# The last products of a hybrid encoder step: another order, the last tiles one by one, and their rows added by VectorE

## The chip, the core and the metric

The kernel runs on one core of one Trainium2 chip. The metric is the device time of one execution in microseconds (us); before the change the median of three runs is 2330.51 us (2329.35 to 2331.84). Five engines work side by side and meet through semaphores: PE (TensorE, matmuls, with its weight loads PEld), DVE (VectorE), ACT (ScalarE), POOL (GpSimd) and SP (SyncE, which here only issues DMAs). Sixteen DMA engines move data; SP, ACT and GpSimd issue to them through queues of their own.

## The reference

One layer of a streaming encoder. The rows are 1024 prompt frames and 8 x 16 sample frames, 1152 rows of 2048 numbers.

```python
h = rms_norm(x, norm_pre)
q_sb, k_sb, v_sb, gate_sb, q_r, k_r, v_r, gate_r = split(h @ w_in)      # 2048 x 8192
o_sb = stick_breaking(q_sb, k_sb, v_sb)       # 8 heads, strictly causal; sample frames also see 1024 cached ones
o_r, state = retention(rope(q_r), rope(k_r), v_r, state)                # 8 heads, chunks of 64
y = concat(head_rms_norm(o_sb) * silu(gate_sb), head_rms_norm(o_r) * silu(gate_r))   # rows x 2048
out = y @ w_out                                                          # 2048 x 2048
x = x + rms_norm(out, norm_post)
```

All inputs and outputs are float32. The change lies in the last two lines: the output projection and the normalised sum.

## The kernel before

**Precision.** Every large matmul is done on float32 pairs: `split` (lines 165 to 169) copies a block into a rounded "high" half on ACT and subtracts it on DVE for the "low" half. `times` (line 1162) then adds high x high, high x low and low x high into one accumulator: three matmuls per block, 128 x 128 against 128 x 512.

**Rows.** Group 0 (G0) holds row tiles 0 to 3 and the sample tile, group 1 (G1) row tiles 4 to 7. Of each group, two tiles of 128 rows are the "upper" half and two the "lower" half.

**The output projection** (from line 1153 on) multiplies 2 x 2 blocks by the seven-product form of Strassen and Winograd. `LEFT` and `RIGHT` (lines 66, 67) say which block, or which precomputed sum of blocks, each product 1 to 7 takes; the sums of weights lie in `s_b`, those of rows in `s_s`, all in HBM. `GOES` (line 69) says for each group and product what is done with its result: a triple of destination block, source block (None: plain copy on ACT), sign or third block (then two blocks are added), and 1 where the destination has its final value. C11 and C12 are the two column halves of the upper rows, C21 and C22 those of the lower rows. Each product comes in two halves, nh 0 and 1, of 512 columns. One pass has up to five accumulators: two tiles of G0, one sample tile (products 1, 2, 3 and 5 alone), two tiles of G1. For each of eight blocks `load_split` (line 1177) loads 256 KB of weights through SP into a ring of five raw buffers (`wr`) and splits them into a ring of four (`wh`, `wl`); then every accumulator takes its three matmuls.

Product 5 of G0 with the sample tile is done earlier, under the last attention heads. Then the loop at line 1335 runs products 1, 2, 6, 7, 5 (G1 alone), 3, and after it product 4. `both` and `left` (lines 1310, 295) load and split a product's left operand one or two half products ahead; `then` (line 1325) says when. G0 alternates between two kept places (`kept`, `at`), G1 between two buffers. In the first half of product 1, G1 runs two blocks behind G0 (`LAG`), since its operand is just being loaded.

**Background jobs.** Work beside the matmuls is written as generators. `tick` (line 222) advances the program's own clock by one and issues one step of one job that is due; a step ends by saying in how many ticks it wants to go on. `product` calls `tick` a given number of times after each accumulator's three matmuls: two in product 1, one later on. `drain` and `all_of` tick until a job is done. `pin` (line 185) keeps an instruction behind the last matmul issued so far (`anchor`) in the order that the scheduler makes; what is not pinned, such as `load_split`, may go ahead as far as its buffers allow. Each engine and each queue then works in its order. The jobs of this stretch are: `sums` with `sum_rows` (the row sums of G1: eight items of two loads, four subtractions on DVE and one store through ACT), `left` and `left_sample`, `load_gpost`, and `collect` (line 1209), which takes an accumulator out of PSUM by `GOES`.

**Finishing rows.** Where `GOES` marks a block as final, `complete` squares it on ACT into a column of the row's sum and multiplies it by the gain on DVE. When all four 512-column parts of a row tile are complete, `finish` (line 1298) makes the inverse root (`scale`, `inv_rms`: small steps on DVE and one root on ACT), scales each part on ACT and has `add_out` store it with an adding DMA from GpSimd: the output rows already hold x, copied there by `residuals` long before. Each part is 256 KB.

**The end.** The second half of product 4 runs three blocks for all four accumulators from the ring. The other five blocks (`KEPT`) are loaded and split into a place of their own (`kh`, `kl`), and each tile in turn takes its last five blocks from there, so that the tiles end one after the other. Each tile's last part is then subtracted, squared and scaled; parts listed in `BY_DVE` are multiplied and added to x on DVE (line 1381), with x loaded in 512-column pieces (`xr`), and stored plainly through SP (`store`, line 1283); the others are scaled on ACT and go through `add_out`.

Of the kernel before, what the change touches and what calls it, by code (L numbers as in the profile page):

```python
# [9 lines left out]
F32 = mybir.dt.float32  # L10
# [52 lines left out]
HT = KT // 2  # L63
HALF = D // 2
KEPT = 5
LEFT = {1: ("y", 0, 0), 2: ("y", 1, 0), 3: ("s", 2), 4: ("y", 1, 1), 5: ("s", 3), 6: ("s", 0), 7: ("s", 1)}
RIGHT = {1: (0, 0), 2: (1, 0), 3: (1, 1), 4: 2, 5: 0, 6: 3, 7: 1}
C11, C12, C21, C22 = (0, 0), (0, 1), (1, 0), (1, 1)
GOES = {
    0: {  # L70
        5: ((C22, None, "+", 0), (C12, None, "+", 0)), 3: ((C12, C12, "+", 1),),
        1: ((C21, None, "+", 0),), 2: ((C11, C21, "+", 1),),
        6: ((C21, C21, "+", 0), (C12, C12, C21, 0)), 7: ((C21, C21, "+", 0), (C22, C22, C21, 1)),
        4: ((C21, C21, "-", 1),),
    },
    1: {
        1: ((C21, None, "+", 0),), 2: ((C11, C21, "+", 1),), 6: ((C12, C21, "+", 0),),
        7: ((C22, C12, "+", 0), (C21, C12, "+", 0)), 4: ((C21, C21, "-", 1),), 5: ((C22, C22, "+", 1), (C12, C12, "+", 0)), 3: ((C12, C12, "+", 1),),
    },
}  # L80
CS1, CS2 = (2, 0), (2, 1)
SAMPLE_LEFT = {5: 0, 3: 1, 1: 0, 2: 1}
# [10 lines left out]
def tile_hybrid_step(  # L93
# [40 lines left out]
    def x_rows(t):  # L134
        return x_prompt[0, t * P : (t + 1) * P, :] if t < PT else xs_flat
# [29 lines left out]
    def split(hi, lo, src):  # L165
        return (
            nc.scalar.activation(hi, src, AF.Copy),  # L167
            nc.vector.tensor_tensor(lo, src, hi.bitcast(F32), ALU.subtract),  # L168
        )
# [271 lines left out]
    with ExitStack() as s1:  # L441
# [713 lines left out]
        def weights_of(n, nh, k):  # L1155
            kind = RIGHT[n]
            if isinstance(kind, int):
                return s_b[nh][k][:, kind, :]
            rows = slice((kind[0] * HT + k) * P, (kind[0] * HT + k + 1) * P)
            return w_out[0, rows, kind[1] * HALF + nh * 512 : kind[1] * HALF + (nh + 1) * 512]  # L1160

        def times(a, x, k, ts, wh, wl, first, last):
            hi, lo = x
            nc.tensor.matmul(a, hi[k][:, ts], wh, start=first, stop=False)  # L1164
            nc.tensor.matmul(a, hi[k][:, ts], wl, start=False, stop=False)  # L1165
            anchor[0] = nc.tensor.matmul(a, lo[k][:, ts], wh, start=False, stop=last)  # L1166

# [41 lines left out]
        def collect(n, nh, accs):  # L1209
            for key, a in accs:  # L1210
                g, p = (0, 0) if key == "s" else key

                def at(block):
                    return (g, 2 * block[0] + p), 2 * block[1] + nh

                for dst, src, how, last in SAMPLE_GOES[n] if key == "s" else GOES[g][n]:
                    o = area(*at(dst))
                    if src is None:
                        nc.scalar.activation(o, a, AF.Copy)
                    elif isinstance(how, str):  # L1220
                        nc.vector.tensor_tensor(o, area(*at(src)), a, ALU.add if how == "+" else ALU.subtract)
                    else:
                        nc.vector.tensor_tensor(o, area(*at(src)), area(*at(how)), ALU.add)
                    if last:
                        Job(complete(*at(dst)), D_FIN)
                    yield 1
# [14 lines left out]
    with ExitStack() as s3:  # L1241
# [18 lines left out]
        def tile_of(key):  # L1260
            return SAMPLE if key[1] == 4 else GROUPS[key[0]]["tiles"][key[1]]
# [43 lines left out]
                yield 1  # L1305
                add_out(key, c)

        at = {2: 0, 6: 1, 7: 0, 3: 1, 4: 0}

        def both(n, groups):  # L1310
            made = []
# [8 lines left out]
        def all_of(made):  # L1320
# [2 lines left out]

        G0, G1, BOTH = (0,), (1,), (0, 1)
        then = {
            (1, 1): ((2, BOTH),), (2, 1): ((6, BOTH),), (6, 0): ((7, BOTH),), (7, 0): ((5, G1), (3, G0)),
            (5, 0): ((3, G1),), (3, 0): ((4, BOTH),),
        }
        (first,) = both(1, G1)
        more = Job(sums(fp, [sum_rows(1, h) for h in range(H)], D_SUM3), 16)  # L1330
# [1 line left out]
        ready = [Job(left_sample(1, *mine["s", 1], fp, "ys", 4), 24)]  # L1332
        for p in range(4):
            outs[1, p] = rp.tile([P, D], F32, name=f"out{p}", tag=f"out{p}")
        for n, groups in ((1, BOTH), (2, BOTH), (6, BOTH), (7, BOTH), (5, G1), (3, BOTH)):
            for nh in range(2):
                if n > 1 and nh == 0:
                    all_of(ready)
                    ready = []
                if (n, nh) == (2, 1):  # L1340
                    drain(more)
                for what in then.get((n, nh), ()):
                    ready += jobs_of(both(*what))
                start = dict(feed=first, lag=LAG) if (n, nh) == (1, 0) else {}
                accs = product(n, nh, groups, n < 4, 2 if n < 2 else 1, **start)
                if (n, nh) == (2, 1):
                    phases.close()
                    xp.append(s3.enter_context(tc.tile_pool(name="xp", bufs=1)))
                Job(collect(n, nh, accs), 1)
        all_of(ready)  # L1350
        Job(collect(4, 0, product(4, 0, BOTH, False, 1)), 1)
        accs = product(4, 1, BOTH, False, 1, HT - KEPT)
        kh, kl = (half[1].rearrange("p a n -> p (a n)").rearrange("p (k n) -> p k n", k=KEPT) for half in mov)
        for k in range(KEPT):
            wr = wp.tile([P, 512], F32, name="wr3", tag="wr", bufs=5)
            nc.sync.dma_start(wr, weights_of(4, 1, HT - KEPT + k))
            split(kh[:, k], kl[:, k], wr)
        while jobs:
            tick()
        scaled = [c3.tile([P, 2, 512], F32, name=f"og{t}", tag=t) for t in ("sh", "sl")]  # L1360
        rows = {}
        BY_DVE = {(0, 0): (1,), (0, 1): (1,), (1, 0): (1, 3), (1, 1): (0, 2, 3, 1)}
        for (g, p), _ in accs:
            for c in BY_DVE[g, p]:
                x = rows[g, p, c] = xp[0].tile([P, 512], F32, name="xr", tag="xr", bufs=8)
                nc.sync.dma_start(x, x_rows(tile_of((g, 2 + p)))[:, c * 512 : (c + 1) * 512])
        for (g, p), a in accs:
            key = g, 2 + p
            for k in range(KEPT):
                k1 = HT - KEPT + k  # L1370
                times(a, mine[g, 4], k1, TS[p], kh[:, k], kl[:, k], False, k1 == HT - 1)
            o = area(key, 1)
            nc.vector.tensor_tensor(o, o, a, ALU.subtract)
            square(key, 1, o)
            t = scaled[g][:, p, :]
            nc.vector.tensor_tensor(t, o, gpost[:, 512:1024], ALU.mult)
            rs = scale(key)
            for c in (0, 2, 3, 1):
                part = t if c == 1 else area(key, c)
                if (g, p, c) in rows:  # L1380
                    nc.vector.scalar_tensor_tensor(part, part, rs, rows[g, p, c], ALU.mult, ALU.add)
                    store(key, c, nc.sync, part)
                else:
                    nc.scalar.activation(part, part, AF.Copy, scale=rs)
                    add_out(key, c)
# [104 lines left out]
```

## Time and profile before

| | |
|---|---|
| median of three runs | 2330.51 us |
| profiled execution | 2331.03 us, of which the span of instructions is 2329.3 us |
| mean granted TensorE clock | 0.992 |
| PE busy | 2264.7 us (97%), 14496 matmuls |
| DVE busy | 1231.3 us (53%) |
| ACT busy | 920.4 us (40%) |
| POOL busy | 362.7 us (16%) |
| DMA | 460.51 MB, mean 198 GB/s |

The page gives busy time by engine, then the span in 40 slices of 58 us, one digit each for tenths of busy time, then the DMA queues (q0 is GpSimd's, q1 SP's, q10 ACT's), the chain of work that ended last, and the costliest groups of instructions. Times in other views are us from the start of the span. A releaser in square brackets names what ended an engine's idle time before an instruction.

### The profile page before, as it was taken

The page shows a single profiled execution, that of the slowest core. Times are in us where ns is not written, and L with a number is a line of the kernel's source. Part 1 is how long each engine was busy: PE and PEld are TensorE (multiplying, and loading weights), DVE is VectorE, ACT ScalarE, POOL GpSimd, SP SyncE. Part 2 cuts the span into 40 slices and gives each one's busy share as a digit, 9 for nine tenths or more (in the row PEclk, how much of TensorE's full clock was granted, in tenths as well). Part 3 has the DMA queues.
Part 4 walks back from the last instruction along what each step waited for, and adds up shares of the span by engine and source line. Part 5 has one row for each costly group of instructions (what it writes and reads, how often), then busy time and mean ns, then how long its engine had stood idle before and what let it go on. Part 6 is the DMA issues. An engine that isn't in the chain of part 4 may idle for free.

```text
span 2329.3 us, 39299 instructions
## 1 busy us (share of the span) xinstructions
PE 2264.7 (97%) x14496; PEld 2045.5 (88%) x14496; DVE 1231.3 (53%) x2540; ACT 920.4 (40%) x1948; POOL 362.7 (16%) x606
## 2 busy tenths in 40 slices
PE   7999999999999999999999999999999999999995
PEld 7999999999999999998888989888888887788884
DVE  7235444353435444355556565655665666555754
ACT  6323333333333333334343334333334445334435
POOL 3002020111202020111102112020211211000004
PEclk9999999999999999999999999999999999999998
DMA  7546657575557647567677787878886767864539
GB/s 256 184 146 193 193 157 213 179 213 167 169 175 209 195 148 221 175 199 255 166 234 205 228 231 225 227 212 226 231 234 199 209 175 187 265 196 157 171 103 181
DMA packets 447073, 460.51 MB, mean 198 GB/s; under 512 B 182048, under 2 KB 310048, under 8 KB 445728
## 3 DMA queue, kind: packets, MB, share of 16 engines
q1 hardware_dynamic: 315808, 292.28, 43.3%
q0 software_dynamic: 29440, 79.72, 12.4%
q10 hardware_dynamic: 101632, 86.00, 11.8%
q8 instruction: 113, 1.85, 0.3%
q14 instruction: 80, 0.66, 0.1%
HBM read 353.02 MB, written 114.29 MB: 201 GB/s over the span
## 4 chain that ended last, share of the span: by engine, by line
PE 83%; DMA 7%; DVE 5%; ACT 3%; issue 2%; SPq 0%; POOL 0%; DVEq 0%; ACTq 0%; POOLq 0%
PE acc L371 45%; PE accn L427 17%; PE a L1165 4%; PE a L1164 4%; PE a L1166 4%; PE pa L752 2%; PE z L722 2%; PE zc L791 1%; PE pd L855 1%; DMA mr<-s_h 1%; DMA yr<-s_y 1%; DMA ro<-s_rk 1%; PE pa L900 1%; DMA s_rk<-rk 1%; DVE kp L651 1%
## 5 line engine op out<-in xcount | busy, mean ns | idle before, releaser
L371 PE MATMUL acc<-mh,wh 128*128 128x256 f32 (+2 forms) x2304 | 662.5, 340 | 0.0
L371 PE MATMUL acc<-ml,wh 128*128 128x256 f32 (+2 forms) x2304 | 658.9, 339 | 0.0
L371 PE MATMUL acc<-mh,wl 128*128 128x256 f32 (+2 forms) x2304 | 656.5, 338 | 0.0
L168 DVE TENSOR_TENSOR wl<-wr,wh 128x512 fp32r<-128x512 f32 x507 | 348.0, 690 | 487.4 <-ACT wh L167 464.8
L167 ACT ACTIVATE wh<-wr 128x512 fp32r<-128x512 f32 x507 | 319.0, 631 | 653.2 <-PE acc L371 347.3
L371 PEld LDWEIGHTS acc<-ml,wh 128*128 128x128 f32 x2304 | 421.7, 188 | 31.2 <-issue 3.3
L371 PEld LDWEIGHTS acc<-mh,wl 128*128 128x128 f32 x2304 | 424.2, 188 | 27.8
L371 PEld LDWEIGHTS acc<-mh,wh 128*128 128x128 f32 x2304 | 420.1, 188 | 31.9 <-issue 3.3
L427 PE MATMUL accn<-whn,mh 128*128 128x256 f32 x1152 | 330.5, 287 | 0.0
L427 PE MATMUL accn<-wln,mh 128*128 128x256 f32 x1152 | 326.5, 283 | 0.0
L427 PE MATMUL accn<-whn,ml 128*128 128x256 f32 x1152 | 326.0, 283 | 0.0
L427 PEld LDWEIGHTS accn<-whn,mh 128*128 128x128 f32 x1152 | 221.5, 192 | 3.2 <-issue 1.1
L427 PEld LDWEIGHTS accn<-wln,mh 128*128 128x128 f32 x1152 | 221.6, 192 | 0.8
L427 PEld LDWEIGHTS accn<-whn,ml 128*128 128x128 f32 x1152 | 221.3, 192 | 0.0
L168 DVE TENSOR_TENSOR wln<-wrn,whn 128x512 fp32r<-128x512 f32 x128 | 87.7, 688 | 147.2 <-ACT whn L167 146.0
L167 ACT ACTIVATE whn<-wrn 128x512 fp32r<-128x512 f32 x128 | 80.7, 633 | 188.3 <-PE accn L427 93.3
L615 POOL DMA_DIRECT2D be<-s_be x128 | 94.1, 741 | 146.6 <-DMA s_be<-be 123.0
L651 DVE TENSOR_TENSOR_SCAN kp<-kp 128x1152 f32<-128x1152 f32 (+4 forms) x40 | 82.7, 2067 | 52.3 <-POOL kp L640 35.7
L640 POOL TENSOR_SCALAR_AFFINE_SELECT kb<-kb 128x128 f32<-128x128 f32 x64 | 30.6, 485 | 458.1 <-ACT kb L634 455.8
L778 POOL DMA_DIRECT2D kcT<-cache_k x64 | 34.6, 545 | 422.4 <-PE pd L855 268.8
L1165 PE MATMUL a<-wl,mh 128*128 128x512 f32 x246 | 96.8, 394 | 2.4 <-DVE wl L168 2.4
L1164 PE MATMUL a<-wh,mh 128*128 128x512 f32 x246 | 96.5, 393 | 2.1 <-DVE rg L454 1.5
(241 smaller groups left out, 2999.9 us busy)
## 6 DMA issues: line engine op xcount, KB each, us to landing
wr<-w_cols SPq DMA_DIRECT2D x384, 256.0 KB, 4.4
wrn<-w_rows SPq DMA_DIRECT2D x128, 256.0 KB, 3.4
kcT<-cache_k POOLq DMA_DIRECT2D x64, 512.0 KB, 8.3
vc<-cache_v SPq DMA_DIRECT2D x64, 512.0 KB, 5.6
wr<-s_b SPq DMA_DIRECT2D x80, 256.0 KB, 3.2
br<-w_out SPq DMA_DIRECT2D x64, 256.0 KB, 5.2
s_b<-br ACTq DMA_DIRECT2D x32, 512.0 KB, 4.6
wr<-w_out SPq DMA_DIRECT2D x48, 256.0 KB, 4.2
```

The costliest lines, as they stand in the source:

```text
L167: nc.scalar.activation(hi, src, AF.Copy),
L168: nc.vector.tensor_tensor(lo, src, hi.bitcast(F32), ALU.subtract),
L371: last = nc.tensor.matmul(a[:, :m], lhs[:, j, :], rhs[w][:, j, o : o + m], start=(w == 0 and j == 0 and n == 0), stop=(w == KT // WQ - 1 a ...
L427: anchor[0] = nc.tensor.matmul(a, lhs[q][:, jj, ts], rhs[:, j, :], start=(w == 0 and j == 0 and n == 0 and t % 2 == 0), stop=(w == KT // 2 ...
L615: q.dma_start(raw[32 * i : 32 * i + 32, :].rearrange("p (k a) -> p k a", a=32), s[:, :, 32 * i : 32 * i + 32].rearrange("k (j b) a -> b (k ...
L651: nc.vector.tensor_tensor_scan(rev, rev, rev, 1.0, ALU.mult, ALU.bypass)
L722: nc.tensor.matmul(z[:, :c], q2[a][:, i * P : (i + 1) * P], k2[b][:, s : s + c], start=(m == 0), stop=(m == 2),)
L752: nc.tensor.matmul(po[:, :P], at[:, j, :], vn[:, j, :], start=(j == 0), stop=(j == t))
L778: ready.append((kc, nc.gpsimd.dma_start(kc, cache_k[h, m // 4, m % 4])))
L1164: nc.tensor.matmul(a, hi[k][:, ts], wh, start=first, stop=False)
L1165: nc.tensor.matmul(a, hi[k][:, ts], wl, start=False, stop=False)
L1166: anchor[0] = nc.tensor.matmul(a, lo[k][:, ts], wh, start=False, stop=last)
```

## The change

The products now run in the order 1, 2, 5 (G1 alone), 3, 6, 7, 4, with the same table `GOES` for both groups; the finality marks move accordingly, so that C12 is final with product 6. `then` and `at` follow the new order. The ticks per accumulator are three in product 1, two in 6 and 7 and in the first half of 4, one elsewhere. Before product 4 the program ticks until the upper rows and the sample rows are finished. During the first half of product 4 a new job, `keep_blocks`, loads and splits all eight weight blocks of the second half: five into the place used before, three (`rest`) into the buffers of two upper row tiles of G0; it then loads x for the first two of the last row tiles, 1 MB each, into buffers of upper rows of G1. The second half of product 4 takes one tile after the other, all eight blocks from the kept weights; the first matmul of each tile is pinned. While a G0 tile starts, x of a G1 tile is loaded. DVE multiplies and adds all parts but column part 0 of the first three tiles, which still go through ACT and an adding store.

```diff
+D_KEEP = 2
 GOES = {
-    0: {
-        5: ((C22, None, "+", 0), (C12, None, "+", 0)), 3: ((C12, C12, "+", 1),),
-        1: ((C21, None, "+", 0),), 2: ((C11, C21, "+", 1),),
-        6: ((C21, C21, "+", 0), (C12, C12, C21, 0)), 7: ((C21, C21, "+", 0), (C22, C22, C21, 1)),
-        4: ((C21, C21, "-", 1),),
-    },
-    1: {
-        1: ((C21, None, "+", 0),), 2: ((C11, C21, "+", 1),), 6: ((C12, C21, "+", 0),),
-        7: ((C22, C12, "+", 0), (C21, C12, "+", 0)), 4: ((C21, C21, "-", 1),), 5: ((C22, C22, "+", 1), (C12, C12, "+", 0)), 3: ((C12, C12, "+", 1),),
-    },
+    5: ((C22, None, "+", 0), (C12, None, "+", 0)), 3: ((C12, C12, "+", 0),),
+    1: ((C21, None, "+", 0),), 2: ((C11, C21, "+", 1),),
+    6: ((C21, C21, "+", 0), (C12, C12, C21, 1)), 7: ((C21, C21, "+", 0), (C22, C22, C21, 1)),
+    4: ((C21, C21, "-", 1),),
 }
...
-        def times(a, x, k, ts, wh, wl, first, last):
+        def times(a, x, k, ts, wh, wl, first, last, held=False):
             hi, lo = x
-            nc.tensor.matmul(a, hi[k][:, ts], wh, start=first, stop=False)
+            ins = nc.tensor.matmul(a, hi[k][:, ts], wh, start=first, stop=False)
+            if held:
+                pin(ins)
...
-        at = {2: 0, 6: 1, 7: 0, 3: 1, 4: 0}
+        at = {2: 0, 3: 1, 6: 0, 7: 1, 4: 0}
...
         then = {
-            (1, 1): ((2, BOTH),), (2, 1): ((6, BOTH),), (6, 0): ((7, BOTH),), (7, 0): ((5, G1), (3, G0)),
-            (5, 0): ((3, G1),), (3, 0): ((4, BOTH),),
+            (1, 1): ((2, BOTH),), (2, 1): ((5, G1), (3, G0)), (5, 0): ((3, G1),), (3, 0): ((6, BOTH),),
+            (6, 0): ((7, BOTH),), (7, 0): ((4, BOTH),),
         }
...
-        for n, groups in ((1, BOTH), (2, BOTH), (6, BOTH), (7, BOTH), (5, G1), (3, BOTH)):
+        for n, groups in ((1, BOTH), (2, BOTH), (5, G1), (3, BOTH), (6, BOTH), (7, BOTH)):
...
-                accs = product(n, nh, groups, n < 4, 2 if n < 2 else 1, **start)
+                accs = product(n, nh, groups, n < 4, {1: 3, 6: 2, 7: 2}.get(n, 1), **start)
...
         all_of(ready)
-        Job(collect(4, 0, product(4, 0, BOTH, False, 1)), 1)
-        accs = product(4, 1, BOTH, False, 1, HT - KEPT)
-        kh, kl = (half[1].rearrange("p a n -> p (a n)").rearrange("p (k n) -> p k n", k=KEPT) for half in mov)
-        for k in range(KEPT):
-            wr = wp.tile([P, 512], F32, name="wr3", tag="wr", bufs=5)
-            nc.sync.dma_start(wr, weights_of(4, 1, HT - KEPT + k))
-            split(kh[:, k], kl[:, k], wr)
-        while jobs:
-            tick()
+        all_of(finishing[key] for key in ((0, 0), (0, 1), (1, 0), (1, 1), (0, 4)))
+        at_end = [half[1].rearrange("p a n -> p (a n)").rearrange("p (k n) -> p k n", k=KEPT) for half in mov]
+        rest = [mp.tile([P, HT - KEPT, 512], F32R, name=f"w{t}", tag=t) for t in ("mh2", "ml2")]
+        keep = [[x[:, k] for k in range(KEPT)] + [y[:, k] for k in range(HT - KEPT)] for x, y in zip(at_end, rest)]
+        LAST = ((0, 0), (0, 1), (1, 0), (1, 1))
+        rows = {
+            key: pool.tile([P, D], F32, name=f"x{i}", tag=tag)
+            for i, (key, pool, tag) in enumerate(zip(LAST, (rp, rp, xp[0], xp[0]), ("out0", "out1", "x2", "x3")))
+        }
+
+        def keep_blocks():
+            for k in range(HT):
+                wr = wp.tile([P, 512], F32, name="wr3", tag="wr", bufs=5)
+                pin(nc.sync.dma_start(wr, weights_of(4, 1, k)))
+                yield 1
+                pin(*split(keep[0][k], keep[1][k], wr))
+                yield D_KEEP
+            for key in LAST[:2]:
+                load_row(key)
+                yield D_KEEP
+
+        def load_row(key):
+            pin(nc.sync.dma_start(rows[key], x_rows(tile_of((key[0], 2 + key[1])))))
+
+        keeping = Job(keep_blocks(), 1)
+        Job(collect(4, 0, product(4, 0, BOTH, False, 2)), 1)
+        drain(keeping)
         scaled = [c3.tile([P, 2, 512], F32, name=f"og{t}", tag=t) for t in ("sh", "sl")]
-        rows = {}
-        BY_DVE = {(0, 0): (1,), (0, 1): (1,), (1, 0): (1, 3), (1, 1): (0, 2, 3, 1)}
-        for (g, p), _ in accs:
-            for c in BY_DVE[g, p]:
-                x = rows[g, p, c] = xp[0].tile([P, 512], F32, name="xr", tag="xr", bufs=8)
-                nc.sync.dma_start(x, x_rows(tile_of((g, 2 + p)))[:, c * 512 : (c + 1) * 512])
-        for (g, p), a in accs:
+        for g, p in LAST:
             key = g, 2 + p
-            for k in range(KEPT):
-                k1 = HT - KEPT + k
-                times(a, mine[g, 4], k1, TS[p], kh[:, k], kl[:, k], False, k1 == HT - 1)
+            if g == 0:
+                load_row((1, p))
+            a = bank()
+            for k in range(HT):
+                times(a, mine[g, 4], k, TS[p], keep[0][k], keep[1][k], k == 0, k == HT - 1, k == 0)
+                if (g, p) == (0, 0):
+                    tick()
+                    tick()
+            if (g, p) == (0, 0):
+                while jobs:
+                    tick()
             o = area(key, 1)
             nc.vector.tensor_tensor(o, o, a, ALU.subtract)
...
             for c in (0, 2, 3, 1):
                 part = t if c == 1 else area(key, c)
-                if (g, p, c) in rows:
-                    nc.vector.scalar_tensor_tensor(part, part, rs, rows[g, p, c], ALU.mult, ALU.add)
+                if c or (g, p) == (1, 1):
+                    x = rows[g, p][:, c * 512 : (c + 1) * 512]
+                    nc.vector.scalar_tensor_tensor(part, part, rs, x, ALU.mult, ALU.add)
                     store(key, c, nc.sync, part)
                 else:
                     nc.scalar.activation(part, part, AF.Copy, scale=rs)
                     add_out(key, c)
```

2 lines of the change are left out of this document (1 added, 1 removed).

## The prediction, made before the changed kernel ran

> **What bounds the kernel now.** I read the page first, then busy time by product, the DMA queues of the end, and the order of time on each engine there.
>
> ```profile
> span 2329.3 us, 39299 instructions
> PE   7999999999999999999999999999999999999995
> PE 83%; DMA 7%; DVE 5%; ACT 3%; issue 2%; SPq 0%; POOL 0%; DVEq 0%; ACTq 0%; POOLq 0%
> ```
>
> TensorE is the bound in 38 of 40 slices and is 83% of the chain that ended last. Only the first and the last slice show it idle for long. The change touches the stretch from product 1 to the end, so I cut that by product (columns: stretch, length, busy us of PE, weight loads, DVE, ACT, POOL with their counts, granted clock, DMA share, GB/s). The borders are counted back from the last matmul: three matmuls on one tile and one weight block take 21.8/32 = 0.68 us.
>
> ```profile
> 1978.90:2012.00 33.10, 29.67 (x119) 22.79 (x118) 16.10 (x41) 12.72 (x33) 2.18 (x4) 0.95 0.79 257
> 2041.00:2068.20 27.20, 26.00 (x115) 21.52 (x116) 9.94 (x18) 7.44 (x14) 0.00 (x0) 1.00 0.70 228
> 2139.00:2160.80 21.80, 21.80 (x98) 18.06 (x97) 15.00 (x31) 10.35 (x24) 0.00 (x0) 1.00 0.58 192
> 2160.80:2182.50 21.70, 21.70 (x98) 17.96 (x97) 11.30 (x19) 6.29 (x12) 0.00 (x0) 1.00 0.31 98
> 2258.70:2280.50 21.80, 21.80 (x98) 18.06 (x97) 12.71 (x30) 11.95 (x26) 1.79 (x2) 1.00 0.48 119
> 2280.50:2302.30 21.80, 21.77 (x97) 17.68 (x95) 12.80 (x44) 15.51 (x35) 12.17 (x14) 1.00 0.96 143
> 2302.30:2329.30 27.00, 0.00 (x0) 0.00 (x0) 10.35 (x34) 8.10 (x17) 10.42 (x12) 0.60 1.00 217
> ```
>
> The first half of product 1 (first row) loses 3.4 us of TensorE time and runs at a mean clock of 0.95, worth another 33.1 x 0.05 = 1.7 us. The second row loses 1.2 us. From there to 2302.3 TensorE has no gap. Then come 27.0 us without a matmul, with DMA at 1.00. What fills the DMA engines there (busy tenths of the 70 us from 2260 in 40 slices; then queue, kind: packets, MB, share of 16 engines, for these 70 us, for 2296 to 2302 and for 2270 to 2275):
>
> ```profile
> DMA  1323241489981898989999999999999999999910
> q0 software_dynamic: 4032, 7.34, 65.5%
> q1 hardware_dynamic: 2304, 4.20, 17.7%
> ...
> q0 software_dynamic: 607, 1.10, 111.1%
> ...
> q1 hardware_dynamic: 360, 0.64, 39.8%
> ```
>
> Queue 0 carries the adding stores that GpSimd issues: 7.34 MB, all 28 of them. Alone they move 1.10 MB in 6 us x 1.111, so one of 256 KB takes all 16 engines 1.6 us; a plain transfer by the last row (0.64 MB in 5 us x 0.398) takes 0.8 us. 28 x 1.6 = 45 us of DMA work begins when the first adding store is issued, and that is late:
>
> ```profile
> POOL out L1293 <- ACT mh L1304: 293.2, 4, 286.8
> L1293 POOL DMA_DIRECT2D out<-mh x9: 832/915/1367, 2274.0 to 2307.9; - x9
> ```
>
> GpSimd idles 286.8 us and starts at 2274.0. 2274 + 45 = 2319, and the eight plain stores (8 x 0.8 = 6.4 us) share the engines: about 2325; the DMA row falls empty one and a half slices before its end, at 2327. So the end is a queue of stores, not arithmetic.
>
> **The change, part by part.**
>
> *Rows finished earlier.* By the written order all upper rows close with product 6 (nh 1) instead of product 3 (nh 1): four half products, 87 us, before the last matmul instead of two, 44 us. The sample rows close with product 3, which has moved from 44 us to 131 us before the last matmul. Their 20 adding stores (16 + 4, 20 x 1.6 = 32 us of DMA) move into products 6, 7 and the first half of 4. What covers them: product 7's own DMA share today is 0.58 and 0.31, that is 12.6 + 6.7 = 19 us of 43.5; with 16 x 1.6 = 26 us it is about full, and a few us may run into product 4 (share 0.48). ACT's 20 scalings and VectorE's extra work lie under TensorE (15.0 of 21.8 us busy at most in those rows). Weight loads get slower there, but they run five raw and four split blocks ahead (each block 2.7 us). Cost to TensorE: 0; without that cover, the DMA excess, a few us.
>
> *The order itself* moves no matmul in or out (48 + 48 for the lone group of product 5, wherever it stands). Group 0 now copies and adds as group 1 does. Each product's left operand still loads one or two half products ahead into the buffer of the product before last. Taken as 0; bounds -1 to +2 from the waits seen at such borders (the 1.2 us above).
>
> *Three ticks per step in product 1* (two before). A tick issues one step of a background job. The heavy one is the row sums: 8 items, each with 4 subtractions two ticks apart, 3 ticks, a store, 6 ticks: 17 ticks. A tick lasted 0.34 us of TensorE time and now lasts 0.227, so an item is due every 3.9 us instead of 5.8. How fast the queues run items when they are pressed (starts of the subtractions of three successive items, and who TensorE then waited for: total, times, longest):
>
> ```profile
> 1990.76 1.80 DVE L288 TENSOR_TENSOR br<-br 128x256 f32<-128x256 f32 x4 [3.07 <-DMA br<-s_y]
> 1996.21 0.42 DVE L288 TENSOR_TENSOR br<-br 128x256 f32<-128x256 f32 x1
> 2002.27 0.43 DVE L288 TENSOR_TENSOR br<-br 128x256 f32<-128x256 f32 x1 [0.77 <-DMA br<-s_y]
> PEld a L1165 <- DVE wl L168: 3.4, 3, 1.8
> ```
>
> One item per 5.5 to 6.1 us, with VectorE waiting for the item's load; the weight splits stand behind those subtractions in VectorE's queue, and TensorE waits for them. That was just enough for 5.8, not for 3.9. From tick 16 to tick 120 (end of the first half) about five items fit beside the sample and gain steps: a lag of 5 x 1.9 = 9.5 us. The lag of two blocks in the G1 tiles leaves one block (3.4 us) of the four split buffers as reserve. So 6.1 us of stall, and 1.7 us of halved clock as today: 7.8 against the present 3.4 + 1.7 = 5.1. I take +2.5. Bounds: -6.3 if the denser steps remove today's losses (5.1 + 1.2), +7.8 with no reserve and a second halved stretch (9.5 + 3.4 - 5.1). Beside it: the Trainium skill ("TensorE: Matmul & The Clock Gate", Part 1: The HAM clock gate) has the clock halve only after an idle window of about 3.4 us; here the longest wait is 1.8 us and the clock fell all the same, so the trace differs. By that rule the term would be 1.7 us less and the time 1.7 us lower.
>
> *Kept weights.* One split's second half on VectorE, one small step and the next, and three multiply-adds:
>
> ```profile
> L168 DVE TENSOR_TENSOR wl<-wr,wh 128x512 fp32r<-128x512 f32 x507 | 348.0, 690 | 487.4 <-ACT wh L167 464.8
> ...
> 2313.68 0.17 DVE L178 RECIPROCAL outr<-outr 128x1 f32<-128x1 f32 x1 [0.33 <-ACT outr L177]
> 2313.87 0.16 DVE L179 TENSOR_TENSOR outu<-outr 128x1 f32<-128x1 f32 x1
> 2314.64 2.08 DVE L1381 SCALAR_TENSOR_TENSOR out<-out,outr,xr 128x512 f32<-128x512 f32 x3
> ```
>
> Eight blocks are loaded and split once, in the first half of product 4, where before three went through the ring and five were kept: the same eight loads, splits and 96 matmuls. They are needed 0.68 us apart from 2280.5 (before, the kept five had until 2288), so all eight must be split by then. Two ticks per step give 64 ticks for some 24 steps of this job and about 25 of others. VectorE's work there today is 12.7 of 21.8 us, plus five splits at 0.69: covered. Blocks 5 to 7 go into the upper rows' buffers, free once their stores landed, about 2260. The row loads follow on SP: 4 x 1 MB, each needed one tile later; nothing but they wait behind them. The pin on each last tile's first matmul only fixes an order that it has anyway. Cost 0, bounds 0 to 5.4 (a whole first tile late).
>
> *Tile by tile.* Each tile ends 24 matmuls (5.4 us) after the one before, instead of 15 (3.4). VectorE per tile: subtract, gain, eight small steps of about 0.19, three multiply-adds at 0.67: some 5.2 us with its waits for ACT, just under 5.4, so the last tile should find it free. Three adding stores are left (column 0 of three tiles, the last about 1 us before the last matmul) and 13 plain ones.
>
> *The end.* The last tile's chain, from rows:
>
> ```profile
> 2299.42 0.67 DVE L1373 TENSOR_TENSOR out<-out,a 128x512 f32<-128x512 f32 x1
> 2300.72 0.18 ACT L1267 ACTIVATION_READ_ACCUMULATOR sq<-out 128x1 f32 x1
> 2313.44 0.20 ACT L177 ACTIVATE outr<-outv 128x1 f32<-128x1 f32 x1 [0.17 <-DVE ogsl L1381]
> 2316.64 0.74 DVE L1381 SCALAR_TENSOR_TENSOR ogsl<-ogsl,outr,xr 128x512 f32<-128x512 f32 x1
> 2317.41 0.33 SPq L1285 DMA_DIRECT2D out<-ogsl  x1
> L1285 SPq DMA_DIRECT2D out<-ogsl x2: 333/433/533, 2313.4 to 2317.4; - x2
> DMA to landing us min/median/max: 6.7/8.5/10.6
> ...
> L595 ACTq DMA_DIRECT2D out<-vn x16: 389/458/772, 184.1 to 1818.7; - x16
> DMA to landing us min/median/max: 2.3/3.2/5.5
> ```
>
> Subtract to sum of squares 1.5 us; reduce and variance 0.4 and a hop 0.1; from the root to the last of four multiply-adds 2313.44 to 2317.38, 3.9: 5.9 us. Then the last store: 10.6 us behind the queue (2317.4 + 10.6 = 2328.0, so 1.3 us of semaphores close the span), 3.2 for the same 256 KB elsewhere (2.3 to 5.5). I take 3.2, as the queue is gone. Tail: 5.9 + 3.2 + 1.3 = 10.4 instead of 27.0; bounds 9.5 and 15.5 (the 6.7 row, and 1.5 us of VectorE lag). [...]
>
> *Sum.* The profiled execution took 2331.0 us with a span of 2329.3; the median of the runs, 2330.5, is 0.5 below it. 2331.0 - 27.0 + 10.4 + 2.5 = 2316.9 against the profiled one, 2316.4 against the median: 2316.5 us, 0.6% less.
>
> **The rivals.**
>
> A. *Product 1 gets lighter* (0.12): the denser steps start the sums' loads before the busiest stretch and today's 6.3 us of losses go. For it: gaps stand in both halves. Against: VectorE's 3.07 us wait for a load is already there at two ticks. 2316.5 - 2.5 - 6.3 = about 2308.
>
> B. *VectorE takes the end over* (0.17): 5.2 against 5.4 us per tile recovers only 0.2 us a tile; if kept splits or the collecting of product 4's first half leave it 5 us late at the first tile, the last ends 4 to 5 us late: 2321. For it: the thin margin; against: its 12.8 of 21.8 us now.
>
> C. *Slower: product 1 is paced by its queue* (0.08). At 2021.16 and 2031.83 the items' subtractions begin 10.7 us apart:
>
> ```profile
> 2021.16 0.42 DVE L288 TENSOR_TENSOR br<-br 128x256 f32<-128x256 f32 x1
> 2031.83 0.42 DVE L288 TENSOR_TENSOR br<-br 128x256 f32<-128x256 f32 x1
> ```
>
> If all eight took that, 8 x 10.7 = 86 us would stand against the 41 us in which their 181 ticks are due; less the reserve of at most 13.6 us and the 6.3 lost now, +25 us: 2331.0 - 27.0 + 10.4 + 25 - 0.5 = 2339. It decides from 16.6 us of added stall. Against: those two items were spread by their ticks, not held by loads; pressed ones took 5.5 to 6.1.
>
> D. *The change doesn't do what it says* (0.08): the upper rows' adding stores are still queued at the last matmul. If half of the 16 are, 8 x 1.6 = 13 us less the 3 us they overlap: 2326. Against: they are due 40 us earlier, and 26 us of DMA fit.
>
> **How the numbers follow.** My forecast has 0.55: 2316.5, its own range 2312 to 2320. The range 2308.5 to 2326 takes in B, most of A and the edge of D and leaves out C. 0.2% (4.7 us) is about what a measurement here tells from no change: faster is the forecast, A, B and a third of D, 0.87; same the rest of D, 0.05; slower C, 0.08.
>
> **What would show it.** Right: the first adding store near 2180, most landed by 2265; 14496 matmuls as before; the last at 2303 to 2306; then about 10 us, with DMA far under 1.00 and the last store landing in 2.3 to 5.5 us; losses of 6 to 9 us in product 1, waiting for split weights behind the sums. Wrong: gaps at the start of the last half product (kept weights late), a last tile whose subtraction starts over 1 us after its last matmul (B), DMA at 1.00 at the end (D), or 15 us lost in product 1 (C).

## The result, and the profile after

The changed kernel takes 2334.32 us (median of 12 runs, 2328.71 to 2341.72), the kernel before 2331.35 us in the runs beside it (median of 12, 2327.41 to 2337.03). The ratio is 1.001 [0.9996, 1.0023]: no difference that can be measured, where 0.6% less was predicted, and 8 us above the top of the range.

From the page after: the span, PE's row of 40 slices, and the chain that ended last by engine.

```profile
span 2335.4 us, 39299 instructions
PE   7999999999999999999999999999999999899997
PE 83%; DMA 8%; DVE 5%; ACT 2%; issue 2%; SPq 1%; POOL 0%; DVEq 0%; ACTq 0%; POOLq 0%
```

The last digit rose from 5 to 7, and the only other after the first that is not a 9 is slice 35, in product 1. Slices of 58 us don't show losses of 4 to 10 us: three of those that follow have one. The same cut by half product as in the prediction (stretch, length, busy us and counts of PE, weight loads, DVE, ACT, POOL, then granted clock, DMA share, GB/s) for the main stretches that are not full: first half of product 1, first half of 2, second half of 6, second half of 7, first half of 4, and what follows the last matmul:

```profile
1977.90:2009.40 31.50, 29.42 (x121) 23.46 (x121) 17.76 (x44) 13.39 (x33) 2.19 (x4) 0.95 0.88 291
2037.70:2071.40 33.70, 28.91 (x121) 23.47 (x120) 10.93 (x20) 9.55 (x18) 0.00 (x0) 0.95 0.33 112
2196.50:2222.00 25.50, 23.69 (x97) 19.09 (x97) 15.25 (x26) 8.98 (x19) 0.00 (x0) 0.93 0.36 111
2243.80:2271.60 27.80, 24.95 (x98) 20.06 (x97) 15.16 (x39) 14.31 (x29) 10.57 (x12) 0.88 1.07 204
2271.60:2303.50 31.90, 24.90 (x97) 18.70 (x96) 17.01 (x28) 12.42 (x26) 0.00 (x0) 0.95 0.62 217
2325.40:2335.40 10.00, 0.03 (x1) 0.00 (x0) 5.31 (x14) 0.93 (x3) 0.00 (x0) 0.75 0.71 199
```

A half product of 96 matmuls needs 96 x 0.2267 = 21.8 us, one of 120 needs 27.2. What a stretch is longer is its loss, idle time and halved clock together: 4.3, 6.5, 3.7, 6.0 and 10.2 us here, taken from the start of its first matmul to the start of the next stretch's (the table below has sums of these before rounding). The end fell from 27.0 to 10.0 us, and three stretches that lost nothing before lose 19.9 us. The chain that ended last shows how (start, length, what; lines left out):

```profile
2251.20 0.60 DVE out L1220
2251.80 0.61 DVE wl L163
2252.46 0.79 PE a L1162
...
2284.01 11.40 DMA wr<-s_b
...
2296.20 0.79 PE a L1159
...
2325.57 0.61 DVE out L1390
```

In product 7 the chain runs through VectorE's collecting (L1220) before it reaches a weight split (wl, L163) and then a matmul. In product 4 it rests 11.4 us on a single load of weights. Both are places that the prediction put at nothing. After 2303.5 TensorE runs through, and the last tile's subtraction starts 0.2 us after the end of the last matmul.

All runs in one table. Loss per stage as above, from the profiled execution; "tail" is the time after the last matmul; the ratio is to the kernel before on the same chip.

| kernel | products 1, 2 | 6, 7 | 4, first half | 4, second | tail | median us | ratio |
|---|---|---|---|---|---|---|---|
| before | 8.0 | 0 | 0 | 0 | 27.0 | 2331.35 | |
| changed | 11.9 | 9.7 | 10.2 | 0 | 10.0 | 2334.32 | 1.001 [0.9996, 1.0023] |
| e1_order | 9.8 | 0 | 0 | 0 | 15.7 | 2322.49 | 0.9948 [0.993, 0.9966] |
| e2_order_ticks | 8.4 | 10.8 | 0 | 0 | 16.0 | 2332.82 | 0.9991 [0.9976, 1.0005] |
| e3_two_ticks | 9.3 | 7.2 | 10.9 | 0 | 10.0 | 2335.46 | 1.0006 [0.9994, 1.0019] |
| e4_one_tick_67 | 10.4 | 0 | 13.5 | 0 | 9.9 | 2331.6 | 0.9989 [0.9976, 1.0002] |
| e5_rows_late | 10.3 | 9.9 | 2.9 | 0 | 9.9 | 2328.6 | 0.9991 [0.9982, 1.0001] |
| e6_own_raw | 11.8 | 8.2 | 3.2 | 0.2 | 13.2 | 2330.39 | 0.999 [0.9976, 1.0004] |
| e7_all_mended | 8.1 | 0 | 9.6 | 6.4 | 9.9 | 2330.37 | 0.9995 [0.9987, 1.0004] |
| e8_mended_on_sp | 7.8 | 0 | 0.9 | 1.9 | 13.2 | 2322.64 | 0.9963 [0.995, 0.9977] |
| e9_rows_one_tick | 7.8 | 0 | 13.8 | 0 | 9.9 | 2328.03 | 0.9981 [0.9973, 0.999] |
| e10_rows_one_tick_67 | 11.6 | 0 | 13.3 | 0 | 10.0 | 2329.61 | 0.9989 [0.9978, 1.0] |
| e11_two_columns_act | 7.5 | 0 | 0.7 | 1.7 | 14.3 | 2320.56 | 0.9957 [0.9944, 0.997] |

A profile is one execution and a median is not: the two differ by up to 8 us (e4: 2339.4 profiled, median 2331.6; that execution reached product 1 at 1988.2, the changed kernel's at 1977.9, with the same program up to there). So causes are read from the losses, each of one execution, and verdicts from the ratios.

### The profile page after: what moved, and what is told of

Same layout as the page of the kernel before. It is cut to its first block, busy times and chain, and to the rows that moved or that the text cites. A ratio compares the mean times of both kernels' runs of the same rounds, so it can differ in the third digit from the quotient of the medians.

```text
span 2335.4 us, 39299 instructions
## 1 busy us (share of the span) xinstructions
PE 2273.8 (97%) x14496; PEld 2050.2 (88%) x14496; DVE 1234.1 (53%) x2541; ACT 920.5 (39%) x1951; POOL 356.9 (15%) x601
## 3 DMA queue, kind: packets, MB, share of 16 engines
q0 software_dynamic: 28720, 78.41, 11.9%
## 4 chain that ended last, share of the span: by engine, by line
PE 83%; DMA 8%; DVE 5%; ACT 2%; issue 2%; SPq 1%; POOL 0%; DVEq 0%; ACTq 0%; POOLq 0%
PE acc L366 46%; PE accn L422 17%; PE a L1162 3%; PE a L1159 3%; PE a L1163 3%; PE pa L747 2%; PE z L717 2%; PE pd L850 1%; PE zc L786 1%; DMA mr<-s_h 1%; DMA yr<-s_y 1%; DMA ro<-s_rk 1%; DMA wr<-s_b 1%; DMA yr<-s_s 1%; DVE wl L163 1%
## 5 line engine op out<-in xcount | busy, mean ns | idle before, releaser
L163 DVE TENSOR_TENSOR wl<-wr,wh 128x512 fp32r<-128x512 f32 x504 | 345.9, 690 | 495.8 <-ACT wh L162 463.7
L163 DVE TENSOR_TENSOR wln<-wrn,whn 128x512 fp32r<-128x512 f32 x128 | 87.6, 688 | 148.2 <-ACT whn L162 146.8
```

## The experiments

### The order alone, and with the ticks

e1 is the kernel before with the order of the products, the `GOES` table, `then` and `at` of the change; ticks and the last half product stay.

```diff
-        for n, groups in ((1, BOTH), (2, BOTH), (6, BOTH), (7, BOTH), (5, G1), (3, BOTH)):
+        for n, groups in ((1, BOTH), (2, BOTH), (5, G1), (3, BOTH), (6, BOTH), (7, BOTH)):
```

> The kernel before with the new order of products alone (one table for both groups, then, at); its old end, two ticks in product 1, one elsewhere. Queue theory (bursts of collecting and finishing steps in VectorE's and ACT's queues, and the kept loads in the ring of raw weights, cost TensorE its time): the ring stays free, so no gap in product 4; gaps at the borders of products 6 and 7 of together 3 to 6 us; product 1 as before; eight adding stores are left at the end, the last matmul near 2307 and the end 14 us later: 2319 to 2324 us. DMA theory (the 20 adding stores under TensorE make the weights late): gaps of 9 us or more there, each ended by a weight load: 2326 us or more.

e2 adds the changed kernel's ticks to e1.

```diff
-                accs = product(n, nh, groups, n < 4, 2 if n < 2 else 1, **start)
+                accs = product(n, nh, groups, n < 4, {1: 3, 6: 2, 7: 2}.get(n, 1), **start)
```

> As e1, with the changed kernel's ticks (three in product 1, two in 6 and 7). Queue theory: 4 us more in product 1 and at the start of product 2, and up to 5 us more at the borders of 6 and 7, so 4 to 9 us above e1. DMA theory: the same stores in the same places, so within 3 us of e1.

Measured: 2322.49 and 2332.82 us. e1 lies in the queue theory's range, though without the gaps of 3 to 6 us that it expected at the borders of 6 and 7; e2 is 10.3 us above e1, a little more than its 4 to 9. The windows of e1 (second halves of 6 and 7, first half of 4, the tail), then the first two of these of e2:

```profile
2197.60:2219.40 21.80, 21.80 (x98) 18.03 (x97) 13.55 (x24) 8.36 (x18) 2.31 (x3) 1.00 0.66 137
2241.10:2262.90 21.80, 21.80 (x97) 18.03 (x97) 15.55 (x39) 13.45 (x28) 6.76 (x9) 1.00 0.90 180
2262.90:2284.70 21.80, 21.80 (x98) 18.05 (x97) 13.07 (x26) 12.83 (x26) 5.86 (x7) 1.00 0.99 213
2306.60:2322.30 15.70, 0.00 (x0) 0.00 (x0) 7.08 (x21) 2.46 (x6) 2.54 (x3) 0.61 0.91 214
```

```profile
2195.80:2221.90 26.10, 23.91 (x97) 19.00 (x96) 15.68 (x27) 9.40 (x20) 0.00 (x0) 0.93 0.42 115
2243.70:2271.90 28.20, 24.82 (x98) 19.96 (x97) 16.33 (x41) 15.57 (x31) 10.42 (x12) 0.88 1.07 207
```

With DMA at 0.66, 0.90 and 0.99, e1's TensorE is busy in every us: the stores moved under products 6, 7 and 4 cost nothing, so the DMA theory falls. So the denser ticks bring the loss (e2 has them in product 1 too; e3 and e4 below take the two apart). What they do is seen in VectorE's order in product 7: first the changed kernel (start, length, instruction, tile; x = several in a row), then e1 at the same place.

```profile
2244.39 0.68 DVE L1218 TENSOR_TENSOR mh<-mh,a 128x512 f32<-128x512 f32 x1
...
2251.12 0.68 DVE L1220 TENSOR_TENSOR out<-out 128x512 f32<-128x512 f32 x1
2251.72 1.89 DVE L163 TENSOR_TENSOR wl<-wr,wh 128x512 fp32r<-128x512 f32 x3
```

```profile
2240.57 0.68 DVE L1215 TENSOR_TENSOR mh<-mh,a 128x512 f32<-128x512 f32 x1
...
2241.77 0.68 DVE L1268 TENSOR_TENSOR out<-out,gpost 128x512 f32<-128x512 f32 x1
2242.37 0.68 DVE L162 TENSOR_TENSOR wl<-wr,wh 128x512 fp32r<-128x512 f32 x1
```

In e1 three collecting and finishing steps stand between two splits there, 1.8 us (a little later four, 2.4 us). With two ticks VectorE does nothing but collecting and finishing steps for 7.3 us (2244.39 to 2251.72, with 0.85 us of waiting for ACT), and then three splits wait at once. VectorE isn't short of time, at 15.2 busy us of 27.8; its order is the matter. TensorE waits, and its clock falls:

```profile
2206.90 0.50 PE L1162 MATMUL a<-wl,mh 128*128 128x512 f32 x1 [1.81 <-DVE wl L163]
2252.46 0.79 PE L1162 MATMUL a<-wl,mh 128*128 128x512 f32 x1 [2.85 <-DVE wl L163]
```

These two waits (the changed kernel) sum to 4.7 us. The mean clocks of 0.93 over 25.5 us and 0.88 over 27.8 us add 1.8 and 3.3 us: together 9.8, the 9.7 lost.

### Which ticks

Each of e3 and e4 changes the table of ticks in the changed kernel: e3 has two in product 1, e4 one in 6 and 7.

```diff
-                accs = product(n, nh, groups, n < 4, {1: 3, 6: 2, 7: 2}.get(n, 1), **start)
+                accs = product(n, nh, groups, n < 4, {1: 2, 6: 2, 7: 2}.get(n, 1), **start)
```

```diff
-                accs = product(n, nh, groups, n < 4, {1: 3, 6: 2, 7: 2}.get(n, 1), **start)
+                accs = product(n, nh, groups, n < 4, {1: 3}.get(n, 1), **start)
```

> The changed kernel with two ticks in product 1 instead of three, the rest unchanged. Queue theory: the 5.2 us wait at the start of product 2 falls to the 1.6 us of before, 4 us faster than the changed kernel: about 2330 us. Rival (the third tick is needed, the sums end too late without it): as the changed kernel or slower, 2334 us or more.

> The changed kernel with one tick in products 6 and 7 instead of two. Queue theory: the steps of collecting and finishing are spread over twice the matmuls, the gaps near 2207 and 2252 us (9 us with the halved clock) shrink by half: 2328 to 2331 us; what isn't finished is issued in one burst ahead of product 4 and may give some of it back. DMA theory: the stores come later and fall into product 4, as slow or slower, 2334 us or more.

Measured: 2335.46 and 2331.6 us, neither told from the kernel before. e3's loss in products 1 and 2 is 2.6 us less than the changed kernel's, and its time isn't: the wait at the start of product 2 fell as the queue theory said (4.8 to 1.7 us), but the time is in the rival's range. In e4 products 6 and 7 lose nothing, so the ticks are the cause of that loss; but the first half of product 4 loses 13.5 us, 3.3 more. Something in the new end waits there at either rate.

### The first half of product 4: rows of x, or the ring

SP's queue in the changed kernel (L1176 loads product 4's own weights, L1361 the kept ones, L1370 rows of x):

```profile
2265.00 0.32 SPq L1176 DMA_DIRECT2D wr<-s_b  x1
2275.94 0.32 SPq L1361 DMA_DIRECT2D wr<-s_b  x1
...
2283.08 0.83 SPq L1370 DMA_DIRECT2D x<-x_prompt  x2
2284.01 1.97 SPq L1176 DMA_DIRECT2D wr<-s_b  x2
2286.03 1.55 SPq L1370 DMA_DIRECT2D x<-x_prompt  x2
```

Two things show. Own and kept blocks take turns in one ring of five raw buffers, and SP stands still from 2265.3 to 2275.9. ACT, which begins each split, stands still itself until 2271.8, at a squaring that waits 7.55 us for VectorE to collect product 7. The last two own blocks are issued at 2284.0, right behind two loads of 1 MB: these two took 11.4 us to land (the chain above), the rows themselves 9.0 to 15.0 us. e5 moves the first two row loads behind all splits; e6 gives the kept blocks two raw buffers of their own, loaded through GpSimd.

```diff
-            for key in LAST[:2]:
-                load_row(key)
-                yield D_KEEP
...
             if g == 0:
+                if p == 0:
+                    load_row((0, 0))
+                    load_row((0, 1))
                 load_row((1, p))
```

```diff
-                wr = wp.tile([P, 512], F32, name="wr3", tag="wr", bufs=5)
-                pin(nc.sync.dma_start(wr, weights_of(4, 1, k)))
+                wr = xp[0].tile([P, 512], F32, name="wk", tag="wk", bufs=2)
+                pin(nc.gpsimd.dma_start(wr, weights_of(4, 1, k)))
```

> The changed kernel, with x for the first two last tiles loaded after the first half of product 4 instead of within it. In the changed kernel that half loses 10.2 us: gaps at 2276.6 (2.0 us), 2285, 2290.4 (2.1) and 2296.2 us (3.0, then a halved clock). Row theory (the 2 MB of x go ahead of the last two weight blocks on SP's queue): the last two gaps go, 4 to 5 us are left, about 2329 us. Ring theory (the kept blocks hold three of the five raw buffers until ACT may split them, so the half's own blocks are loaded too late whatever else is on the queue): 8 us or more are left, 2332 us or more.

> The changed kernel, with two raw buffers of their own for the kept blocks, which GpSimd's queue loads; the rows of x stay. Ring theory: the ring serves the half's own eight blocks alone, and it loses under 3 us instead of 10.2: about 2327 us. Row theory: the 2 MB of x are still there, 6 us or more are lost: 2331 us or more.

Measured: 2328.6 and 2330.39 us. Each takes the first half of product 4 from 10.2 us to about 3, so each looks like the cause, and they don't add. e6 has a longer tail, 13.2 us.

### Both, with fewer ticks

e7 takes e5's and e6's edits together, with two ticks in product 1 and one from 2 to 7. e8 is e7 with the kept blocks loaded through SP.

```diff
-                pin(nc.gpsimd.dma_start(wr, weights_of(4, 1, k)))
+                pin(nc.sync.dma_start(wr, weights_of(4, 1, k)))
```

> The changed kernel with own raw buffers and GpSimd's queue for the kept blocks (e6), the rows of x late (e5), two ticks in product 1 and one elsewhere before product 4. Queue theory: product 1 loses 9 us as in e1 and e3, products 6 and 7 nothing as in e1 and e4, product 4 under 2 us, the end takes the 10 us of the changed kernel: last matmul 2304 to 2307, 2315 to 2319 us, below e1. If something else in the new end costs TensorE its time: 2322 us or more.

> As e7, but the kept blocks' own raw buffers are loaded through SP's queue. If what counts is the place in the ring: as e7. If the order in SP's queue counts (a kept load that waits for its buffer holds up the half's own loads behind it): product 4's first half loses 5 to 10 us again, 2321 to 2328 us.

Measured: 2330.37 and 2322.64 us, intervals apart: the issuing engine decides. In e7 GpSimd's queue has the kept loads (L1361) among adding stores (L1290):

```profile
2260.22 1.40 POOL L1361 DMA_DIRECT2D wk<-s_b  x2
2271.81 3.56 POOL L1290 DMA_DIRECT2D out<-out  x4 [10.19 <-ACT out L1301]
...
2283.53 1.18 POOL L1361 DMA_DIRECT2D wk<-s_b  x2 [7.00 <-DVE ml L163]
2292.42 1.14 POOL L1361 DMA_DIRECT2D wk<-s_b  x2 [7.71 <-DVE ml L163]
```

The first two kept loads are issued behind four adding stores and take up to 10.0 us to land (at most 7.6 us for any kept load in e8). ACT waits 7.5 us for the first of them before it scales the rows of the next four stores. So these stores wait 10.2 us for ACT, the loads behind them wait too, and the last kept blocks come at 2292.4, after the half product that needs them has begun (its first matmul starts at 2289.2). The Trainium skill ("DMA: Bandwidth & Descriptors", Issuing engines are not separate DMA queues) says that issuing from several engines saves only the time of issuing, usually small. Here the choice of engine made 7.7 us between medians: what counts is what stands ahead of a load, in that engine's own order or in its DMA queue; which of the two weighs more stays open.

e7 went by its last sentence. e8's time lies in the second of its ranges, 2321 to 2328 us, but by luck: the first half of product 4 loses 0.9 us there, not 5 to 10.

In e8 losses under TensorE are 10.6 us against the changed kernel's 31.8, but the tail is 13.2 us, and rival B shows. VectorE ahead of the first last tile (L1218 collects, L1271 multiplies by the gain, L1390 is the last subtraction):

```profile
2286.19 0.69 DVE L163 TENSOR_TENSOR wml<-wk,wmh 128x512 fp32r<-128x512 f32 x1 [2.61 <-ACT wmh L162]
2286.80 0.68 DVE L1218 TENSOR_TENSOR mh<-mh,a 128x512 f32<-128x512 f32 x1
...
2291.60 0.68 DVE L1390 TENSOR_TENSOR mh<-mh,a 128x512 f32<-128x512 f32 x1
```

And the group of its last two subtractions (durations, first and last start):

```profile
L1390 DVE TENSOR_TENSOR out<-out,a x2: 676/678/679, 2301.9 to 2307.3; 128x512 f32<-128x512 f32 x2
```

The last kept split ends at 2286.9, 6.7 us after the half product that needs it has begun; eight steps follow that collect the first half's tiles and multiply them by the gain, and the first subtraction starts at 2291.60. From there to 2307.3 are three tiles of 5.2 us each, so a late start is hardly made good: the last subtraction is 3.3 us behind its matmuls, which ended at 2304.0.

### The ring by itself, the bursts by themselves, and the margin

e9 is the changed kernel with late rows and `{1: 2}` as its table of ticks, e10 with late rows and `{1: 3}`; both keep the ring. So e9 differs from e8 by the raw buffers alone, and e10 from e5 by the ticks in 6 and 7 alone. e11 is e8 with one more column part of each of the first three last tiles on ACT and an adding store:

```diff
-                if c or (g, p) == (1, 1):
+                if c in (1, 3) or (g, p) == (1, 1):
```

> The changed kernel with the row loads late (as in e5), two ticks in product 1 and one everywhere between product 2 and product 7; the kept weights stay in the ring. Burst theory (two ticks in products 6 and 7 put the collecting and finishing steps in clumps ahead of the weight splits) with the row theory: TensorE loses 8 to 10 us in product 1 and the start of 2, nothing in 6 and 7, about 3 us in the first half of product 4; the last matmul at about 2305 and 10 us behind it, so about 2316 us. Rival (the loss only moves): with one tick the finishing steps run into product 4, whose first half loses 10 us and more again as in e4, about 2325. Rival B (VectorE late at the first tile): 3 us more behind the last matmul, about 2319.

> As e5 (three ticks in product 1, row loads late), but one tick per accumulator in products 6 and 7. Burst theory: the 9.9 us that e5 lost in 6 and 7 are gone and nothing takes their place: about 2319 us, with 10 to 12 us lost in products 1 and 2. Rival (the loss only moves into product 4): about 2328, as e5. Against e9 it prices the third tick of product 1: 0 to 2.5 us by what e1 to e3 showed, 2.5 us by the prediction.

> As e8 (late rows, kept blocks in raw buffers of their own, dense ticks in none of 6 and 7), but column parts 0 and 2 of the first three last tiles are scaled by ACT and stored with an adding DMA, in place of part 0 alone. VectorE per tile falls from about 5.2 to 4.5 us against 5.4 us of matmuls. If rival B's margin is what makes the 13.2 us behind e8's last matmul, the last subtraction starts about 1.2 us after its matmuls in place of 3.3, the tail is about 11 us and the time 2 us below e8's, about 2320.5. If the adding stores set the end, the tail stays at 13 us or grows.

Measured: 2328.03, 2329.61 and 2320.56 us. e9 and e10 went by the rival: products 6 and 7 lose nothing and the first half of product 4 loses 13 to 14 us. e10 differs from e4 by the late rows alone, and that half loses 13.3 against 13.5 us: with one tick SP issues the rows after the last own load anyway (in e4 from 2291.5 on). So late rows helped e5 alone, and the row theory doesn't explain these losses. SP in e9, then ACT's splits of its first five kept blocks (durations, first and last start), then SP in e8 (own loads, kept loads):

```profile
2238.30 0.32 SPq L1361 DMA_DIRECT2D wr<-s_b  x1
2241.30 0.32 SPq L1176 DMA_DIRECT2D wr<-s_b  x1
2243.64 4.03 SPq L1361 DMA_DIRECT2D wr<-s_b  x2
2249.07 0.32 SPq L1176 DMA_DIRECT2D wr<-s_b  x1
2262.20 0.87 SPq L1361 DMA_DIRECT2D wr<-s_b  x2
```

```profile
L162 ACT ACTIVATE mh<-wr x5: 614/615/633, 2257.3 to 2268.2; 128x512 fp32r<-128x512 f32 x5
```

```profile
2237.65 19.01 SPq L1176 DMA_DIRECT2D wr<-s_b  x8
2256.71 23.23 SPq L1361 DMA_DIRECT2D wk<-s_b  x8
```

In e9 the loads of three kept blocks are issued by 2247.7, but the first of them is split at 2257.3: they hold three of five raw buffers for up to 19 us, SP issues nothing from 2249.4 to 2262.2, and product 4 (from 2255.7) gets its own weights late. In e8 all eight own loads are issued by 2256.7. The first half of product 4, e9 and then e8:

```profile
2255.70:2291.20 35.50, 27.67 (x98) 20.48 (x97) 19.27 (x36) 15.74 (x32) 3.83 (x5) 0.86 0.85 226
```

```profile
2257.50:2280.20 22.70, 22.09 (x98) 17.93 (x97) 15.25 (x30) 13.71 (x30) 6.02 (x7) 1.00 0.90 188
```

That is 13.8 against 0.9 us under TensorE. In time less of it is left, since e8 pays 3.3 us more in the tail and 1.9 in the second half: the medians are 5.4 us apart, but the ratios, 0.9981 [0.9973, 0.999] and 0.9963 [0.995, 0.9977], overlap a little. e11, which has buffers of its own too, is apart from e9: 0.9957 [0.9944, 0.997].

e11's subtractions, and the landing of its last six stores; below them those six of the changed kernel:

```profile
L1390 DVE TENSOR_TENSOR out<-out,a x2: 679/680/680, 2297.6 to 2302.2; 128x512 f32<-128x512 f32 x2
```

```profile
DMA to landing us min/median/max: 6.3/6.4/8.8
```

```profile
DMA to landing us min/median/max: 2.5/2.7/4.8
```

VectorE's lateness goes as expected, from 3.3 to 1.1 us (2302.2 against the last matmul's end at 2301.1). But with three more adding stores the plain ones land in 6.3 to 8.8 us, and the tail is 14.3 us, not 11, with DMA at 0.90 in it (0.79 in e8's): the queue of stores is back. So e11's median meets the expected 2320.5 us by luck. It is the lowest of all, but e11, e8 and e1 have overlapping intervals: each is 0.4 to 0.5% faster than the kernel before, with an interval apart from the changed kernel's, and none is shown best. The order alone (e1) is shown to pay; the new end isn't shown to add to it.

## Why the prediction was wrong, point by point

- **The end: right.** 10.0 us for 10.4. Subtraction to last store 2325.6 to 2331.4, 5.8 us for 5.9; the landing 2.5 to 4.8 us for 3.2. Rival D fell: the first adding store left at 2185.6 and the upper rows' last four at 2260.2.
- **Rows finished earlier, and the order: right.** e1 shows both at nothing under TensorE with DMA at up to 0.99, and takes 11.3 us off the tail by themselves.
- **Three ticks in product 1: near in size by luck, wrong in place.** The prediction put the losses of products 1 and 2 before the change at 6.3 us; counted by matmul starts they are 8.0, and the changed kernel's are 3.9 more. Six kernels with three lose 8.4 to 11.9 us in products 1 and 2, mean 10.7; seven with two lose 7.5 to 9.8, mean 8.3: +2.4 for the predicted +2.5. But it isn't the splits behind the sums. The first half of product 1 got lighter (4.3 for 6.5), and the loss stands at the start of product 2, where PE waits for ACT to take an accumulator of product 1 out (2.7 to 4.8 us in the six, 1.2 to 2.1 in the seven):

```profile
PE a L1159 <- ACT ml L1216: 4.8, 1, 4.8
```

  Shortly before, ACT itself waits 3.0 us for the load of a left operand; what makes that load late stays open. Pairs of medians don't separate so little (e3 against the changed kernel, e9 against e10). Rivals A and C both fell.
- **Two ticks in products 6 and 7: the step that failed first.** The prediction named them in no term. It counted VectorE's busy share ("15.0 of 21.8 us busy at most in those rows") and the split blocks in reserve, and not how many steps a doubled rate puts between two splits: 7.3 us without a split. It cost TensorE 9.7 us; with one tick (e4 against the changed kernel, e10 against e5) the loss is 0. The times of e4 and e10 did not follow, since the first half of product 4 then loses 13 us. Where that half has no kept loads, the denser ticks, the third of product 1 included, make 10.3 us of time (e2 against e1).
- **"The same eight loads, splits and 96 matmuls … Cost 0, bounds 0 to 5.4": the second.** Counting the work was right; its place in the ring was not looked at. Blocks loaded ahead and split late hold raw buffers that product 4's own weights need: 10.2 us in the changed kernel, 13.8 in e9, 0.9 with buffers of their own.
- **"Nothing but they wait behind them": wrong too.** The held-up own loads were issued behind 2 MB of rows and took 11.4 us. Neither theory has it alone: with the rows as early and raw buffers of their own for the kept blocks e6 loses 3.2 us, and with late rows and the shared ring e5 loses 2.9 and e9 13.8. In the changed kernel how much of the 10.2 us belongs to which isn't settled, since either edit alone removes 7.
- **Rival B** didn't happen in the changed kernel, but it did in e6 and e8, where it cost 3.2 us for the predicted 4 to 5. There the last kept split starts 4 and 6 us after the last half product has begun, and VectorE collects only behind it. In e7 it is late as well, but there TensorE loses 6.4 us in that half itself. In the changed kernel, as in e5 and e9, the last one is done before that half begins.

The sum again with what was measured: 2329.3 (span) - 17.0 (tail) + 3.9 (products 1 and 2) + 9.7 (6 and 7) + 10.2 (4) - 0.6 (product 1 began earlier) = 2335.5, for a span of 2335.4.

## What to carry to other kernels

A background rate is a cost of its own: look not at an engine's busy share but at the longest run of background steps between two pieces of work that the bound engine waits for. Work moved earlier through a shared ring is free only if its buffers are given back as fast as they are taken: ask for each load moved ahead when its consumer runs, and who needs that buffer until then. When two edits each remove most of a loss, test both in a kernel where the other suspects are gone before naming either.

## What the runs showed of the hardware

TensorE's clock can halve after a wait of 1.8 to 2.9 us, and it need not. A wait of 1.81 us (2206.90) is followed by matmuls 0.41 us apart, not 0.227:

```profile
2207.46 0.61 PE L1159 MATMUL a<-wh,mh 128*128 128x512 f32 x1
2207.87 0.63 PE L1162 MATMUL a<-wl,mh 128*128 128x512 f32 x1
```

By the windows, the clock took back 1.8 us there and 3.3 us after the wait of 2.85 us, as much again as the waits themselves. In the first half of product 4 of the same execution two waits as long as the first did not bring it down; the granted clock is 1.00 from 2273 to 2296:

```profile
2276.56 0.50 PE L1162 MATMUL a<-wl,mh 128*128 128x512 f32 x1 [1.89 <-DVE wl L163]
2290.38 0.73 PE L1159 MATMUL a<-wh,mh 128*128 128x512 f32 x2 [1.95 <-ACT wh L162]
```

The Trainium skill ("TensorE: Matmul & The Clock Gate", Part 1: The HAM clock gate) has the clock fall after at least one idle window of about 3.4 us; the longest single wait here was shorter in both places where it fell, so the trace differs. So a wait of that length for weights cost its own length here or about twice that, and the length alone doesn't tell which. In e8's first half of product 4, with 0.9 us lost in all, the clock stayed at 1.00.
